# A seventh early set of weight sums, one more pair with seven products, and two sets of sums loaded ahead

## The chip, the cores and the metric

The kernel runs on one core of a Trainium2 chip. The core has a matrix engine (TensorE, PE in the profile), a vector engine (VectorE, DVE), an activation engine (ScalarE, ACT), GpSimd (POOL) and SyncE (SP), which here only issues DMA transfers. The engines run their own instruction streams and wait for one another through semaphores. The metric is the device time of one execution, in microseconds (us), as the median of several runs.

## What is computed

The reference is one layer of a decoder trunk, with 256 tokens, a model width D = 2048 and a branch width E = 4096:

```
h = rmsnorm(x, norm_g)
shift, scale, gate = split(silu(c) @ ada_w + ada_b, 3)
h = h * (1 + scale) + shift
b_gate, c_gate, v, g = split(h @ w_in, 4)        # w_in is 2048 x 16384
u = causal_depthwise_conv(c_gate * v, conv_w)    # three taps
y = b_gate * u * silu(g)                         # 256 x 4096
out = rmsnorm(x + gate * (y @ w_out), final_g)   # w_out is 4096 x 2048
```

All numbers are float32.

## The kernel before

**Products.** Each float32 operand of a large product is split into a high part, rounded to the matrix engine's fp32r format, and a low part, the remainder. ACT makes the high part (a copy, L389 or L1032), DVE the low part (a subtraction, L394 or L1035). A product is then three matmuls: high by high, high by low, low by high.

**Stages.** The kernel makes the conditioning sums and half of the input product's columns first (`plan`, `part`). Then comes the other half (L843): 8 column groups of 8 pieces each, so 64 pieces. A piece loads 1 MB of w_in, ACT and DVE split it, and PE runs 48 matmuls of 128x256 on it. Three tiles each for the raw, high and low parts go round in rings (`w_tile`), so a piece's load goes out when the piece three before it has been split. Beside the first 32 pieces DVE also sums the gate's part of ada_w (`gate_piece`, `gate_sums`, tiles `at_g` and `gacc`). After each piece `early_weights` is called, and counts its calls; L881 calls it once more at the end.

**Output product.** y @ w_out has four parts: the first columns (0 to 1023), the second columns (1024 to 2047) for twelve of the sixteen pairs of row blocks, and two closing parts for the rows of pairs 4 to 7 (`third_products`, `out_mm`). A pair is 2 x 128 rows of w_out by 1024 columns: four blocks of 128x512, b0 to b3. By the ordinary way (`Columns.eight`) a pair takes eight products of 128x128 by 128x512, 24 matmuls. For the pairs in `SEVEN` and `SEVEN_2` it takes seven, 21 matmuls (`Columns.seven`), by Winograd's form of Strassen's scheme. That needs sums of y's blocks (`token_forms`, made once for pairs 8 to 15) and four sums of w_out's blocks: b1 - b0, b2 - b0, b2 + b1 - b0, and b3 minus the third. The sums and the blocks b1 to b3 are split into high and low parts each.

**Where the weight sums come from.** For some pairs DVE makes them on the spot (`sums_of`, three operations). For the units in `UNITS` they are made early, beside the 64 pieces: `EARLY` says at which call of `early_weights` the blocks are loaded, the sums follow one call later, and ACT's queue stores them to DRAM (`store_made`, 1 MB). There are two ways to do it. The ordinary one takes tiles of the raw and low rings (`raw_u`, `sums_u`). The other, for the units in `IN_PLACE`, takes two tiles of 128x1024 that are free at that time (`staged`), sums in place with four operations (`sums_in_place`), and stores three calls after the load; the first two sums then stand in swapped order, which `swapped` undoes.

**Order.** In the output product each engine's order is the written order (`in_order`). Per pair that is: the loads on SyncE (`piece`), the splits on ACT and DVE, the loads of `load_ends(n)`, a step of the first columns' closing (`closing_steps`; none at n = 6), and PE's matmuls. The second columns take their pairs in the order 0, 1, 10, 2, 11, 3, 9, 12, 8, 13, 14, 15, as n = 0 to 11. Their raw blocks and their sums share a ring of four "lo" tiles, high parts a ring of three, low parts a ring of three. A load goes out when DVE has split what stood in its tile. `third_load` and `gated_load` take slots of y's that are finished (`slot`, a pool of 18 places).

Of the kernel before, what the change touches and what calls it, by code (L numbers as in the profile page):

```python
# [30 lines left out]
SLOT = 2048  # L31
# [86 lines left out]
def short_conv_layer(ctx: ExitStack, tc: tile.TileContext, x, c, norm_g, ada_w, ada_b, w_in, conv_w, w_out, final_g, out):  # L118
    nc = tc.nc
# [29 lines left out]
    def w_tile(kind, name, dtype=F32, i=None):  # L149

        if i is None:
            size = 4 if kind in fourth else 3
            i = nth[kind] % size
            nth[kind] = i + 1
        if i == 3:
            return hpool.tile([P, SLOT + 64], dtype, tag=fourth[kind], name=name)[:, 16 : 16 + SLOT]
        return wpool.tile([P, SLOT], dtype, tag=f"{kind}{i}", name=name, bufs=1)
# [253 lines left out]
    def split(raw, n, lo_tag="lo"):  # L411

        return split_lo(raw, n, split_hi(raw, n), lo_tag)
# [82 lines left out]
    sums = {}  # L496
# [238 lines left out]
    EP = 4  # L735
    W = 512
    SEVEN = range(8, 16)
    SEVEN_2 = range(9, 16)
    forms = {}
    ended_silu = [None]  # L740

# [29 lines left out]
        )  # L771

    LAST = (2, 3)
    UNITS = ((0, 15),) + tuple((2 * W, j) for j in (10, 11, 12, 14, 15))
    EARLY = {32 + 4 * i: unit for i, unit in enumerate(UNITS)}
    IN_PLACE = UNITS[0:6:2]
    EARLY.update({55: "gate", 56: ("gated", LAST[0]), 60: ("gated", LAST[1])})
    made = {}
    to_do = []
# [3 lines left out]
    def sums_of(b, s):  # L783

        yield nc.vector.tensor_tensor(  # L785
            out=s[:, 0:2], in0=b[:, 1:3], in1=b[:, 0:1].to_broadcast([P, 2, W]), op=ALU.subtract
        )
        yield nc.vector.tensor_tensor(out=s[:, 2], in0=b[:, 2], in1=s[:, 0], op=ALU.add)
        yield nc.vector.tensor_tensor(out=s[:, 3], in0=b[:, 3], in1=s[:, 2], op=ALU.subtract)  # L789
# [53 lines left out]
    for ct in range(NS, NCT, 2):  # L843
        for q in QUARTERS:
            bank = psum.tile([P, CT, T], F32, tag="mm", name="mm_b")[:, 0:2]
            col = q * E + ct * P
            for kp in range(0, KT, KP):
                raw = raw_tile("raw")
# [55 lines left out]
    def load_ends(n):  # L904

        if n == 1:
            both = hpool.tile([P, TT, HD], F32, tag="b0", name="xr")
            xh.append([both[:, t] for t in range(TT)])
            closing.append(hpool.tile([P, D], F32, tag="b2", name="closing"))
            fourth["lo"] = "b1"  # L910
            load_broadcast(HD, gate_row[0:1, 0:HD])
            load_x(0, 0)
        elif n == 2:
            load_fg(0)
        elif n == 3:
            load_x(0, 1)
        elif n in (5, 6):
            if n == 5:
                xh.append([slot([P, 2 * W], f"xr{t}") for t in range(TT)])
            load_x(1, n - 5)  # L920
        elif n == 7:
            last_gate.append(slot([P, 2 * W], "last_gate"))
            nc.sync.dma_start(last_gate[0], gate_row[0:1, HD:D].partition_broadcast(P))
        elif n == 10:
            thirds.append(third_load(LAST[0]))
        elif n == 11:
            load_fg(1)
            thirds.append(third_load(LAST[1]))

# [5 lines left out]
            load_o(raw, ep * EP + 2 * i, 2, 2 * W, W)  # L935
        return halves_

    def gated_load(ep):
        halves_ = [slot([P, 2 * W], "raw_y") for _ in range(2)]
        for i, raw in enumerate(halves_):  # L940
            nc.sync.dma_start(raw, made["gated", ep][:, i * 2 * W : (i + 1) * 2 * W])
        return halves_

    def split_halves(raws):
# [33 lines left out]
    def weighted(t, c0, n, pr, at):  # L978
# [3 lines left out]
        nc.scalar.activation(pr, r, AF.Square, scale=D**-0.5, accum_out=fsq[:, t, at : at + 1])  # L982
        yield nc.vector.tensor_tensor(out=r, in0=r, in1=closing[0][:, c0 : c0 + n], op=ALU.mult)

    class Columns:


# [5 lines left out]
        def piece(self, n):  # L993


            j, c0 = self.order[n], self.c0
            raw = w_tile("raw" if n == 0 and c0 == 0 else "lo", "raw_o")
            if n == 0 and c0 == 0:
                nth.update({"raw": 0, "lo": 0})
            ready = (c0, j) in made  # L1000
            if ready:
                blocks = raw.rearrange("p (b f) -> p b f", f=W)
                e = 2 * j * P
                nc.sync.dma_start(blocks[:, 1], w_out[0, e : e + P, c0 + W : c0 + 2 * W])
                nc.sync.dma_start(blocks[:, 2:4].rearrange("p b f -> p (b f)"), w_out[0, e + P : e + 2 * P, c0 : c0 + 2 * W])
            else:
                load_o(raw, 2 * j, 2, c0, 2 * W)
            if j in self.in_turn:
                sums = w_tile("lo", "sums_o")
                if ready:  # L1010
                    nc.sync.dma_start(sums, made[c0, j])
                return self.seven(j, raw, sums, ready)
            hi, lo = split(raw, SLOT, "raw")
            return lambda: self.eight(n, j, hi, lo)
# [12 lines left out]
        def seven(self, j, raw, sums, ready):  # L1027


            hi, lo = hi_tile(), lo_tile("raw")  # L1030
            b, s, bh, bl = (v.rearrange("p (b f) -> p b f", f=W) for v in (raw, sums, hi, lo))
            nc.scalar.copy(bh[:, 1:4], b[:, 1:4])  # L1032
            if not ready:
                list(sums_of(b, s))
            nc.vector.tensor_tensor(out=bl[:, 1:4], in0=b[:, 1:4], in1=bh[:, 1:4].bitcast(F32), op=ALU.subtract)  # L1035
            sh, sl = (v.rearrange("p (b f) -> p b f", f=W) for v in split(sums, SLOT, "raw"))
            bank, p1, p6, p75 = self.bank, self.p1, self.p6, self.p75
            opens, last = j == self.in_turn[0], j == self.in_turn[-1]
            swapped = int((self.c0, j) in IN_PLACE)

            def f(i):
                return [forms[j][h][:, i] for h in range(2)]

            def products():
                triple(p1, y_parts(2 * j, 0), bh[:, 1], bl[:, 1], opens, last)
                triple(bank(0, 1), y_parts(2 * j + 1, 0), bh[:, 3], bl[:, 3])
                triple(bank(0, 0), f(3), bh[:, 2], bl[:, 2])
                triple(p75[:, 0], f(2), sh[:, 1 - swapped], sl[:, 1 - swapped], opens, last)
                triple(p75[:, 1], f(0), sh[:, swapped], sl[:, swapped], opens, last)
                triple(p6, f(1), sh[:, 2], sl[:, 2], opens, last)  # L1050
                triple(bank(1, 1), y_parts(2 * j + 1, 1), sh[:, 3], sl[:, 3])

            return products
# [80 lines left out]
    with in_order():  # L1134
        fourth.update({"lo": "b0", "hi": "b1", "raw": "b2"})
        p75 = wide_bank("mm_7")
        wide = [wide_bank("mm_w") for _ in range(TT)]
        first = Columns(
            0, (0, 1, 8, 2, 9, 3, 10, 4, 11, 5, 12, 13, 6, 14, 15, 7), SEVEN,
            lambda t, d: wide[t][:, d], *extra_banks(), p75, True,  # L1140
        )
        for n in range(16):
            if n == 13:
                fourth.clear()
            first.piece(n)()

        second = Columns(2 * W, (0, 1, 10, 2, 11, 3, 9, 12, 8, 13, 14, 15), SEVEN_2, lambda t, d: halves[d][:, t], None, None, None, False)
        products0 = second.piece(0)
        first.gather()
        products1 = second.piece(1)  # L1150
        load_ends(1)
        evict(0)
        halves = [wide_bank("mm_o") for _ in range(2)]
        products0()
        evict(1)
        second.p75 = wide_bank("mm_7")
        second.p1, second.p6 = po = extra_banks()
        products1()
        steps = closing_steps()
        for n in range(2, 12):  # L1160
            products = second.piece(n)
            load_ends(n)
            if n != 6:
                next(steps, None)
            products()
        assert next(steps, None) is None
        gated = [gated_load(LAST[0])]
        third0 = third_piece(LAST[0], thirds[0])
        second.gather()
        third_products(*third0)  # L1170
        third_products(*third_piece(LAST[1], thirds[1]))
        gated.append(gated_load(LAST[1]))
        late = []
        for t, ep in enumerate(LAST):
            hi, lo = split_halves(gated[t])
            move(t)
            low_halves(gated[t], hi, lo)
            late.append((ep, hi, lo))
        for ep, hi, lo in late:
            out_mm(po[0], 0, ep, hi, lo)  # L1180
        third(0)
        third_weighted(0)
        third(1)
        for t in range(TT):
            nc.scalar.activation(ends[t][:, 1], po[t], AF.Square, scale=D**-0.5, accum_out=fsq[:, t, 2:3])
            finish(t)
            if t == 0:
                third_weighted(1)
                for ep, hi, lo in late:
                    out_mm(po[1], 1, ep, hi, lo)  # L1190
# [24 lines left out]
```

## Time and profile before

| | us |
|---|---|
| median of 3 runs (900.93 to 901.40) | 901.32 |
| the profiled execution | 902.04 |
| its span, first to last instruction | 900.3 |
| start of the 64 pieces on PE | 376.0 |
| start of the first columns | 725.7 |
| start of the second columns | 807.3 |
| end of PE's last matmul | 892.7 |

The profile is that of one execution. Its span is 1.7 us shorter than that execution's time, the rest lying before the first and after the last instruction. The four lower rows are from the chain of work that ended last. Engine names and lines are those of the kernel printed above. In a row of the timeline the first number is the start in us from the span's beginning, the second the length; a bracket says how long the engine was idle before and who released it. PE's matmuls overlap one another, so the distance of their starts is their price, not their length.

### The profile page before, as it was taken

Reading aid. Unit: us, or ns where it says so; the run is one execution under the profiler, and the core shown is the slowest. Engines: PE = TensorE matmul, PEld = TensorE weight load, DVE = VectorE, ACT = ScalarE, POOL = GpSimd, SP = SyncE. Lnnn points to the kernel's source line nnn. Section 1 sums busy time; section 2 is a strip of 40 time slices with the busy share of each in tenths; the row PEclk is TensorE's granted clock in tenths of the full one; section 3 lists DMA queues with packets and bytes.
Section 4 is the critical chain, followed back from the end, with each engine's and each line's share of the span. In section 5 each row is a group of like instructions: output and inputs, shape, how many; then the busy total and the mean of one; then the engine's idle time right before and its main releaser. Section 6 shows DMA issues by size and latency. Waiting matters only on the chain.

```text
span 900.3 us, 16556 instructions
## 1 busy us (share of the span) xinstructions
PE 885.1 (98%) x6974; PEld 847.0 (94%) x6974; DVE 698.7 (78%) x704; ACT 492.9 (55%) x441; POOL 94.0 (10%) x108
## 2 busy tenths in 40 slices
PE   7999999999999999999999999999999999999996
PEld 4999999999999999999999999999999988888875
DVE  5899988889888866856965587677767688877986
ACT  6768866665558856644343434344534455455553
POOL 0000000010000223420033002430000000000000
PEclk9999999999999999999999999999999999999999
DMA  9999999999998597876877788999898765489862
GB/s 310 370 370 368 368 331 361 335 365 377 374 322 288 163 293 226 244 223 198 287 235 229 253 288 270 314 303 327 283 314 285 267 234 191 170 300 365 280 258 93
DMA packets 165817, 257.29 MB, mean 286 GB/s; under 512 B 7844, under 2 KB 106756, under 8 KB 164336
## 3 DMA queue, kind: packets, MB, share of 16 engines
q1 hardware_dynamic: 160192, 239.89, 80.3%
q0 software_dynamic: 3840, 7.94, 3.3%
q10 hardware_dynamic: 1712, 8.43, 2.3%
q8 instruction: 54, 0.88, 0.4%
q14 instruction: 19, 0.16, 0.1%
HBM read 237.86 MB, written 10.50 MB: 276 GB/s over the span
## 4 chain that ended last, share of the span: by engine, by line
PE 89%; DMA 5%; DVE 3%; ACT 1%; issue 1%; SPq 0%; ACTq 0%; DVEq 0%
PE mm_s L554 39%; PE mm_b L554 34%; PE mm_w L969 7%; PE mm L969 5%; PE mm_o L969 4%; DMA at<-in_ada_w_dram 2%; DMA raw<-in_sc_w_in_dram 2%; DVE lo L394 1%; ACT hi L389 1%; DMA sums_o<-made 1%; DMA raw_u<-in_sc_w_out_dram 1%; DVE staged L798 0%; PE sum L427 0%; SPq L247 0%; DVE sums_u L785 0%
## 5 line engine op out<-in xcount | busy, mean ns | idle before, releaser
L554 PE MATMUL mm_b<-hT,hi 128*128 128x256 f32 x2048 | 348.5, 276 | 0.0
L554 PE MATMUL mm_s<-hT,hi 128*128 128x256 f32 x2048 | 335.8, 277 | 0.0
L554 PEld LDWEIGHTS mm_b<-hT,hi 128*128 128x128 f32 x2048 | 308.0, 188 | 0.0
L554 PEld LDWEIGHTS mm_s<-hT,hi 128*128 128x128 f32 x2048 | 298.4, 188 | 0.3
L554 PE MATMUL mm_b<-hT,lo 128*128 128x256 f32 x1024 | 283.0, 276 | 0.6 <-DVE lo L394 0.5
L554 PE MATMUL mm_s<-hT,lo 128*128 128x256 f32 x1024 | 261.3, 276 | 0.0
L389 ACT CAST hi<-raw 128x2048 fp32r<-128x2048 f32 (+1 forms) x66 | 123.8, 1875 | 181.2 <-PE mm_b L554 80.4
L394 DVE TENSOR_TENSOR lo<-raw,hi 128x2048 fp32r<-128x2048 f32 (+1 forms) x66 | 149.7, 2269 | 70.1 <-ACT hi L389 68.7
L554 PEld LDWEIGHTS mm_b<-hT,lo 128*128 128x128 f32 x1024 | 192.2, 188 | 1.2 <-DVE lo L394 1.2
L554 PEld LDWEIGHTS mm_s<-hT,lo 128*128 128x128 f32 x1024 | 182.4, 188 | 0.0
L394 DVE TENSOR_TENSOR lo<-raw_s,hi 128x2048 fp32r<-128x2048 f32 (+1 forms) x80 | 148.8, 1866 | 31.0 <-ACT hi L389 30.4
L389 ACT CAST hi<-raw_s 128x2048 fp32r<-128x2048 f32 (+2 forms) x81 | 124.1, 1541 | 68.3 <-PE mm_s L554 44.3
L524 DVE SCALAR_TENSOR_TENSOR gv<-at,silu_c,gv 128x512 f32<-128x512 f32 x105 | 78.8, 750 | 9.0 <-DMA at<-in_ada_w_dram 7.3
L578 ACT COPY acc<-mm_s 128x1024 f32<-128x1024 f32 x54 | 54.5, 1012 | 29.7 <-PE mm_s L554 29.6
L730 POOL TENSOR_TENSOR gacc<-gacc,z 128x512 f32<-128x512 f32 x28 | 48.7, 1741 | 115.9 <-DMA z<-gacc 115.9
L969 PE MATMUL mm_w<-hi,y 128*128 128x512 f32 x160 | 52.0, 389 | 0.0
L724 DVE SCALAR_TENSOR_TENSOR gacc<-at_g,silu_c,gacc 128x512 f32<-128x512 f32 x60 | 45.0, 749 | 6.4 <-DMA at_g<-in_ada_w_dram 5.1
L969 PE MATMUL mm_o<-hi,y 128*128 128x512 f32 x140 | 45.7, 390 | 0.0
L389 ACT CAST hi<-sums_o 128x2048 fp32r<-128x2048 f32 x15 | 28.6, 1910 | 30.8 <-DVE sums_o L789 12.2
L394 DVE TENSOR_TENSOR lo<-sums_o,hi 128x2048 fp32r<-128x2048 f32 x15 | 34.4, 2292 | 13.7 <-ACT hi L389 13.7
L592 ACT COPY mm_s<-acc 128x1024 f32<-128x1024 f32 x38 | 38.6, 1016 | 2.6 <-DVE acc L581 1.8
L394 DVE TENSOR_TENSOR lo<-raw_o,hi 128x2048 fp32r<-128x2048 f32 x13 | 29.8, 2290 | 9.4 <-ACT hi L389 9.4
(191 smaller groups left out, 755.7 us busy)
## 6 DMA issues: line engine op xcount, KB each, us to landing
raw<-in_sc_w_in_dram SPq DMA_DIRECT2D x64, 1024.0 KB, 7.3
raw_s<-in_sc_w_in_dram SPq DMA_DIRECT2D x47, 1024.0 KB, 8.5
at<-in_ada_w_dram SPq DMA_DIRECT2D x126, 256.0 KB, 8.0
raw_o<-in_sc_w_out_dram SPq DMA_DIRECT2D x22, 1024.0 KB, 5.3
raw_s<-in_sc_w_in_dram SPq DMA_DIRECT2D x33, 512.0 KB, 7.2
at_g<-in_ada_w_dram SPq DMA_DIRECT2D x32, 512.0 KB, 8.6
sums_o<-made SPq DMA_DIRECT2D x6, 1024.0 KB, 6.0
raw_u<-in_sc_w_out_dram SPq DMA_DIRECT2D x5, 1024.0 KB, 6.2
```

The source lines that it names most:

```text
L389: last_high[0] = nc.scalar.copy(hi[:, :n], raw[:, :n])
L394: last_low[0] = nc.vector.tensor_tensor(out=lo[:, :n], in0=raw[:, :n], in1=hi[:, :n].bitcast(F32), op=ALU.subtract)
L524: nc.vector.scalar_tensor_tensor(out=gv, in0=at4[:, i], scalar=c_k, in1=gv, op0=ALU.mult, op1=ALU.add)
L554: mm = last_mm[0] = nc.tensor.matmul(dst, w, h[k], start=begins and left, stop=ends, skip_group_check=True)
L578: nc.scalar.copy(acc[ch, q], bank)
L592: nc.scalar.copy(bank, acc[ch, q])
L724: nc.vector.scalar_tensor_tensor(out=ga, in0=at3[:, i, :], scalar=s, in1=ga, op0=ALU.mult, op1=ALU.add)
L730: nc.gpsimd.tensor_tensor(out=ga, in0=ga, in1=turned, op=ALU.add)
L969: nc.tensor.matmul(dst, y[a], b, start=opens and i == 0, stop=ends and i == 2, skip_group_check=True)
```

## The change

```diff
-    SEVEN_2 = range(9, 16)
+    SEVEN_2 = range(8, 16)
...
-    UNITS = ((0, 15),) + tuple((2 * W, j) for j in (10, 11, 12, 14, 15))
-    EARLY = {32 + 4 * i: unit for i, unit in enumerate(UNITS)}
-    IN_PLACE = UNITS[0:6:2]
+    UNITS = ((0, 15),) + tuple((2 * W, j) for j in (8, 10, 11, 12, 14, 15))
+    EARLY = {28 + 4 * i if i else 24: unit for i, unit in enumerate(UNITS)}
+    IN_PLACE = UNITS[0:1] + UNITS[1:6:2]
...
-        elif n == 10:
+        elif n in (9, 10):
+            ahead[2 * W, n + 5] = load_made((2 * W, n + 5))
+        elif n == 11:
             thirds.append(third_load(LAST[0]))
-        elif n == 11:
             load_fg(1)
             thirds.append(third_load(LAST[1]))
...
-    def gated_load(ep):
+    def load_made(unit):
         halves_ = [slot([P, 2 * W], "raw_y") for _ in range(2)]
         for i, raw in enumerate(halves_):
-            nc.sync.dma_start(raw, made["gated", ep][:, i * 2 * W : (i + 1) * 2 * W])
+            nc.sync.dma_start(raw, made[unit][:, i * 2 * W : (i + 1) * 2 * W])
         return halves_
...
             if j in self.in_turn:
+                if (c0, j) in ahead:
+                    return self.seven(j, raw, ahead[c0, j], ready)
                 sums = w_tile("lo", "sums_o")
...
-            sh, sl = (v.rearrange("p (b f) -> p b f", f=W) for v in split(sums, SLOT, "raw"))
+            if isinstance(sums, list):
+                parts = split_halves(sums)
+                low_halves(sums, *parts)
+            else:
+                parts = split(sums, SLOT, "raw")
+            sh, sl = (v.rearrange("p (b f) -> p b f", f=W) for v in parts)
```

- Pair 8 of the second columns goes over from eight products to seven. Its sums are made early, in place.
- The units' calls: (0, 15) moves from 32 to 24, pair 8 takes 32, and the other five stay at 36, 40, 44, 48 and 52. (0, 15), pair 8, pair 11 and pair 14 are made in place.
- The sums of pairs 14 and 15 are loaded by `load_ends(9)` and `load_ends(10)`, one pair ahead, into two slots of y's each, and no longer by `piece` into a tile of the "lo" ring. They are split in halves (`split_halves`, `low_halves`: two operations each on ACT and DVE).
- The first `third_load` moves from n = 10 to n = 11.

More of the change, by code (lines that the diff above doesn't have):

```diff
@@ L983, in weighted @@
         yield nc.vector.tensor_tensor(out=r, in0=r, in1=closing[0][:, c0 : c0 + n], op=ALU.mult)
+    ahead = {}
     class Columns:
@@ L1030, in seven @@
             hi, lo = hi_tile(), lo_tile("raw")
-            b, s, bh, bl = (v.rearrange("p (b f) -> p b f", f=W) for v in (raw, sums, hi, lo))
+            b, bh, bl = (v.rearrange("p (b f) -> p b f", f=W) for v in (raw, hi, lo))
             nc.scalar.copy(bh[:, 1:4], b[:, 1:4])
             if not ready:
-                list(sums_of(b, s))
+                list(sums_of(b, sums.rearrange("p (b f) -> p b f", f=W)))
             nc.vector.tensor_tensor(out=bl[:, 1:4], in0=b[:, 1:4], in1=bh[:, 1:4].bitcast(F32), op=ALU.subtract)
-            sh, sl = (v.rearrange("p (b f) -> p b f", f=W) for v in split(sums, SLOT, "raw"))
+            if isinstance(sums, list):
[4 more added lines that the diff above has]
+            sh, sl = (v.rearrange("p (b f) -> p b f", f=W) for v in parts)
             bank, p1, p6, p75 = self.bank, self.p1, self.p6, self.p75
@@ L1166, in short_conv_layer @@
         assert next(steps, None) is None
-        gated = [gated_load(LAST[0])]
+        gated = [load_made(("gated", LAST[0]))]
         third0 = third_piece(LAST[0], thirds[0])
@@ L1171, in short_conv_layer @@
         third_products(*third_piece(LAST[1], thirds[1]))
-        gated.append(gated_load(LAST[1]))
+        gated.append(load_made(("gated", LAST[1])))
         late = []
```

## The prediction

> **What bounds the kernel now.** I read the busy shares first, then the waits of TensorE (PE), then the chain that ended last, and only then the timelines of the two stretches that the change touches. The page's busy list and its chain by engine:
>
> ```profile
> PE 885.1 (98%) x6974; PEld 847.0 (94%) x6974; DVE 698.7 (78%) x704; ACT 492.9 (55%) x441; POOL 94.0 (10%) x108
> ...
> PE 89%; DMA 5%; DVE 3%; ACT 1%; issue 1%; SPq 0%; ACTq 0%; DVEq 0%
> ```
>
> PE is busy for 98% of the span, so time can go in two ways only: fewer matmuls, or fewer waits of PE. The view of waits lists what PE waited for (total us, times, longest); two lines lie in this change's stretches:
>
> ```profile
> PE mm L969 <- DVE lo L394: 1.9, 2, 1.7
> ...
> PE mm_b L554 <- DVE lo L394: 0.5, 2, 0.3
> ```
>
> The first is the output product, the second the input product. Here is the price of one 128x512 matmul, and the start of the input product's last 64 pieces, from the chain (start, length, count):
>
> ```profile
> 376.01 173.98 PE mm_b L554 x1535
> ...
> 870.21 11.56 PE mm_o L969 x51
> ```
>
> 11.56/51 = 0.227 us a matmul. 173.98/1535 x 48 = 5.44 us a piece, so piece n begins at 376.01 + 5.4375 n. PE's timeline in the second columns (start, length):
>
> ```profile
> 843.65 0.39 PE L969 MATMUL mm<-hi,y 128*128 128x512 f32 x1
> ...
> 853.88 0.39 PE L969 MATMUL mm<-hi,y 128*128 128x512 f32 x1
> ...
> 856.57 0.50 PE L969 MATMUL mm<-lo,form 128*128 128x512 f32 x1 [0.25 <-DVE lo L394]
> ...
> 863.96 0.39 PE L969 MATMUL mm<-hi,y 128*128 128x512 f32 x1
> ...
> 868.10 0.50 PE L969 MATMUL mm<-lo,form_h 128*128 128x512 f32 x1 [1.70 <-DVE lo L394]
> ...
> 870.50 0.62 PE L969 MATMUL mm_o<-hi,y 128*128 128x512 f32 x2
> ```
>
> Pair 12 opens at 843.65 and has 21 matmuls, so pair 8 opens at 848.41 and, with 24, ends at 853.88, where pair 13 opens. Pair 15 opens at 863.96, waits 1.70 us at its eleventh matmul, and ends at 870.73 (the row of 870.50 holds its last matmul and the next piece's first).
>
> **The waits' cause.** Pair 15's sums are the cause of the 1.70 us. SyncE's issues, and then ACT's splits:
>
> ```profile
> 838.32 3.06 SPq L768 DMA_DIRECT2D raw_o<-in_sc_w_out_dram  x2
> ...
> 856.54 0.33 SPq L1011 DMA_DIRECT2D sums_o<-made  x1
> ```
>
> ```profile
> 843.85 1.91 ACT L389 CAST hi<-raw_o 128x2048 fp32r<-128x2048 f32 x1 [1.07 <-PE mm_o L969]
> ...
> 863.81 1.91 ACT L389 CAST hi<-sums_o 128x2048 fp32r<-128x2048 f32 x1 [2.93 <-DMA sums_o<-made]
> ```
>
> The load goes out at 856.54, when VectorE (DVE) has finished with the "lo" tile that it overwrites, and ACT gets it at 863.81. DVE's timeline around it (start, length, line, what idled before it):
>
> ```profile
> 845.02 1.22 DVE L976 TENSOR_TENSOR xr<-xr,z 128x1024 f32<-128x1024 f32 x1
> 846.15 2.29 DVE L394 TENSOR_TENSOR lo<-raw_o,hi 128x2048 fp32r<-128x2048 f32 x1
> 848.36 1.22 DVE L983 TENSOR_TENSOR xr<-xr,closing 128x1024 f32<-128x1024 f32 x1
> 849.49 1.22 DVE L785 TENSOR_TENSOR sums_o<-raw_o 128x1024 f32<-128x1024 f32 x1
> ...
> 852.08 1.75 DVE L1035 TENSOR_TENSOR lo<-raw_o,hi 128x1536 fp32r<-128x1536 f32 x1
> 854.22 2.29 DVE L394 TENSOR_TENSOR lo<-sums_o,hi 128x2048 fp32r<-128x2048 f32 x1 [0.39 <-ACT hi L389]
> 856.43 1.75 DVE L1035 TENSOR_TENSOR lo<-raw_o,hi 128x1536 fp32r<-128x1536 f32 x1
> 858.10 2.29 DVE L394 TENSOR_TENSOR lo<-sums_o,hi 128x2048 fp32r<-128x2048 f32 x1
> 860.91 1.76 DVE L1035 TENSOR_TENSOR lo<-raw_o,hi 128x1536 fp32r<-128x1536 f32 x1 [0.53 <-ACT hi L1032]
> 865.75 2.29 DVE L394 TENSOR_TENSOR lo<-sums_o,hi 128x2048 fp32r<-128x2048 f32 x1 [3.08 <-ACT hi L389]
> 867.96 2.35 DVE L953 TENSOR_TENSOR lo<-raw_y,hi 128x1024 fp32r<-128x1024 f32 x2
> ```
>
> Two things are to be seen. DVE has a hole of 3.08 us ahead of pair 15's sums. But from 845.02 to 856.43 it is full but for 0.39 us, and it feeds pair 13 with nothing to spare: the low halves of pair 13's blocks end at 853.83, and PE wants them one matmul after 853.88.
>
> **Part one: pair 8 with seven products.** It removes three matmuls, 3 x 0.227 = 0.68 us. On DVE the one split of 2.29 us becomes a split of the three blocks (1.75) and one of the sums (2.29). By start-to-start steps of these rows, 1.67 is added (856.43 to 858.10). ACT gets one more split and has room. DVE's order is written out by hand, so everything behind pair 8 slides. I walk it:
>
> - Pair 8's blocks: DVE 846.15 to 847.82. ACT splits them from 843.85; the "hi" tile for the sums comes free with pair 12's ninth matmul (843.65 + 9 x 0.227 = 845.7, about 845.9 with its drain), so ACT ends at about 847.85.
> - Pair 8's sums: DVE 847.9 to 850.1; PE wants them at 848.41 + 10 x 0.227 = 850.7. No wait.
> - Closing step L983 to 851.25; pair 13's sums (849.49 to 852.08, 2.59) to 853.85; its blocks to 855.55.
> - PE ends pair 8 at 848.41 + 21 x 0.227 = 853.17 and wants pair 13's low halves at 853.40: **a new wait of 2.2 us**. ACT splits pair 13's sums 853.9 to 855.8, DVE 855.85 to 858.1; PE wants them at 857.7: 0.4 more. The eleventh matmul starts at 858.15; in before it started at 856.57, so pair 13 closes 1.6 us later than now, at 860.8 (859.2 now).
>
> **Part two: the sums of 14 and 15 ahead.** SyncE issues them behind the blocks of pairs 13 and 14, into slots of finished y's. Each is split in halves: 2.35 us on DVE instead of 2.29 (row 867.96). DVE is then ready with pair 14's blocks at 859.8, its sums at 862.2, pair 15's blocks at 864.2, its sums at 866.6. PE wants these at 861.0, 863.1, 865.8 and 867.9. The 1.70 us are gone, and pairs 14 and 15 run 4.76 each: 860.8 + 9.52 = 870.3, against 870.73 now. **These two parts give 0.4 us**, of the 0.68 + 1.70 + 0.25 = 2.6 that PE alone would allow. The rest goes into the wait at pair 13. Behind 870 DVE is about as early as before, so the 0.4 reaches the end.
>
> **Part three: the seventh set, early.** The two 512 KB loads go out behind piece 24's load, about 484 (the split at 508.44 is piece 26's, as shown below; piece 24's load follows piece 21's split, 5 x 5.44 us ahead of that split's end). The old load's place at piece 32 now serves pair 8 and costs what it cost. New are the loads, four DVE operations, and a 1 MB store on ACT's queue behind piece 27's split. The windows by piece (length, busy of PE, PEld, DVE, ACT, POOL, clock, DMA share, GB/s); the group of DVE's operation on `staged` (ns, least, median, most); DVE's rows; and SyncE's:
>
> ```profile
> 501.10:506.50 5.40, 5.40 (x50) 5.40 (x49) 2.29 (x1) 1.87 (x2) 0.00 (x0) 1.00 0.61 196
> 506.50:511.90 5.40, 5.40 (x50) 5.40 (x49) 5.14 (x8) 2.94 (x3) 0.00 (x0) 1.00 0.92 276
> 511.90:517.40 5.50, 5.50 (x50) 5.50 (x50) 2.79 (x5) 1.91 (x1) 0.00 (x0) 1.00 1.04 360
> 517.40:522.80 5.40, 5.40 (x50) 5.40 (x49) 5.02 (x6) 2.40 (x2) 0.00 (x0) 1.00 0.81 263
> 522.80:528.30 5.50, 5.50 (x51) 5.50 (x51) 2.20 (x2) 1.97 (x2) 0.00 (x0) 1.00 0.96 320
> ```
>
> ```profile
> L798 DVE TENSOR_TENSOR staged<-staged x12: 680/684/692, 554.1 to 643.5; 128x512 f32<-128x512 f32 x12
> ```
>
> ```profile
> 508.44 2.29 DVE L394 TENSOR_TENSOR lo<-raw,hi 128x2048 fp32r<-128x2048 f32 x1
> ...
> 528.86 1.54 DVE L724 SCALAR_TENSOR_TENSOR gacc<-at_g,silu_c,gacc 128x512 f32<-128x512 f32 x2 [3.86 <-DMA at_g<-in_ada_w_dram]
> 530.32 2.28 DVE L394 TENSOR_TENSOR lo<-raw,hi 128x2048 fp32r<-128x2048 f32 x1
> ...
> 558.99 2.28 DVE L394 TENSOR_TENSOR lo<-raw,hi 128x2048 fp32r<-128x2048 f32 x1
> ```
>
> ```profile
> 532.63 0.37 SPq L849 DMA_DIRECT2D raw<-in_sc_w_in_dram  x1
> ```
>
> The loads are wanted by 505 and have DMA engines at 0.61 before that, so they cost nothing. The four operations are 4 x 0.684 = 2.7 us of DVE from about 505. They push the split at 508.44 by 2.7 at worst, to an end at 513.4; it serves piece 26, which begins at 517.4. Hidden, with 4 us left; without that cover they would cost 2.7. The store meets full DMA engines (1.04). 1.05 MB at that window's 360 GB/s are 2.9 us, which loads in flight pay. The next window has 0.19 x 5.4 = 1.0 us free, so 1.9 us are left for the gate's load that DVE already waits 3.86 us for at 528.86. Behind that in DVE's order is the split at 530.32, which ends at 532.60, just ahead of SyncE's load at 532.63 into the tile that it freed. That is piece 32's, so the split is piece 29's. PE wants it at 376.01 + 29 x 5.4375 + 0.23 = 533.9: 1.3 us of margin, and a wait of 1.9 - 1.3 = 0.6. The ends are 0, if the store falls into gaps, and 2.9, if the delay lasts to piece 34: its split (558.99) ends at 561.3 and its products begin at 376.01 + 34 x 5.4375 + 0.2 = 561.1, with no margin at all. Below nothing there is no end, since nothing is taken away ahead of piece 32. I take 0.6: the row nearest the store is the split with the 1.3 us.
>
> The sum: -0.4 + 0.6 = **+0.2 us**. The profiled execution took 902.04 (span 900.3), which would be 902.2. The runs' median is 901.32, 0.7 lower; the same difference gives 901.5, which I predict.
>
> **The rivals.**
>
> - *The whole 2.6 us* (898.7, or 899.3 with the 0.6). This needs DVE to be ready for pair 13 at 853.4. For it speaks the hole of 3.08 us; against it, that the hole lies behind pair 13 and the order is fixed. Chance 0.10.
> - *Slower by the store's backlog.* The delay of 2.9 us is not worked off before piece 34, since the windows to 528 are 0.8 to 1.0 full, and PE pays it all: 901.3 - 0.4 + 2.9 = 903.8. It decides from a delay of 2.2 us there (1.8 beside the 0.4). Against it speaks that some share is free in most windows. [...] Chance 0.14.
> - *Pair 8's sums come late.* They go out when the tile of pair 9's sums is free, about 841, where SyncE's second load of the row at 838.32 goes now. Two rows of the DMA view (KB, us to landing), the issues at 832.93 and at 812.91:
>
> ```profile
> sums_o<-made SPq DMA_DIRECT2D x1, 1024.0 KB, 4.8
> ...
> sums_o<-made SPq DMA_DIRECT2D x1, 1024.0 KB, 9.8
> ```
>
>   With 4.8 they are there at 845.8, in time. With 9.8 they land at 850.8 where ACT wants them at 845.9: 4.9 late, DVE and PE with them, 901.5 + 4.9 = 906.4. Chance 0.04.
> - *The sums ahead are not ahead:* the y slots come free only with pair 8, at 853. Pair 14's blocks, queued behind on SyncE, would then land near 858, and DVE be ready at 861, when PE wants them. This costs about nothing and lies inside the forecast.
>
> The forecast has 0.72. This kernel's measurement can tell about 0.2%, 1.8 us, from no change: faster 0.10, within 0.72, slower 0.14 + 0.04 = 0.18. The forecast's own bounds are 0 to 0.9 us gained at the end (a dozen hand-overs of about 0.04 us in the walk, either way), and 0 to 1.6 us for the store (a delay of 2.9 against 1.3): 900.4 to 902.9. To hold 8 in 10 the range reaches part of the way to the first two rivals: 899.8 to 903.4.
>
> **What would show it.** Step one: 21 matmuls for pair 8, and a wait of some 2.2 us at pair 13's second matmul; no wait there means that DVE was not full. Step two: no wait on pair 15's sums. Step three: pieces 29 to 39 begin later by what the store costs; the output product's start, 725.7 in the table above, tells it. The prediction is wrong if that start moves by over 2 us or pair 13 does not wait.

## The result and the profile after

The changed kernel takes 902.55 us (median of 20 runs, 901.29 to 904.40), the kernel before 901.21 in the same comparison (20 runs, 899.35 to 903.09). The ratio is 1.0018, 95% interval 1.0011 to 1.0025: 1.3 us more, where 0.2 more was forecast. Ten of the 20 runs stand between 901.3 and 902.2 and ten between 902.9 and 904.4, which the kernel before does not do. Of all the runs below, three took 1114, 3191 and 4424 us (in kernels 5 and 6 and the kernel before) and are in no ratio. The profiled execution (901.85, span 900.1) is of the lower group.

First the page's busy line of the changed kernel, and its waits of PE (total us, times, longest):

```profile
PE 883.8 (98%) x6971; PEld 846.7 (94%) x6971; DVE 704.6 (78%) x711; ACT 494.6 (55%) x444; POOL 91.4 (10%) x108
```

```profile
PE mm L970 <- DVE lo L1040: 2.4, 1, 2.4
PE mm L970 <- DVE lo L394: 1.1, 2, 0.8
```

The 1.7 us at pair 15 are gone, and a wait of 2.4 us has come, on the split of a pair's blocks (L1040, L1035 before). PE's three waits, and then DVE's timeline from pair 12's sums on:

```profile
850.31 0.50 PE L970 MATMUL mm<-lo,gate 128*128 128x512 f32 x1 [0.77 <-DVE lo L394]
...
855.70 0.51 PE L970 MATMUL mm<-lo,y 128*128 128x512 f32 x1 [2.37 <-DVE lo L1040]
...
858.37 0.50 PE L970 MATMUL mm<-lo,form 128*128 128x512 f32 x1 [0.30 <-DVE lo L394]
```

```profile
843.72 1.22 DVE L977 TENSOR_TENSOR xr<-xr,z 128x1024 f32<-128x1024 f32 x1
844.86 1.75 DVE L1040 TENSOR_TENSOR lo<-raw_o,hi 128x1536 fp32r<-128x1536 f32 x1
847.96 2.29 DVE L394 TENSOR_TENSOR lo<-sums_o,hi 128x2048 fp32r<-128x2048 f32 x1 [1.35 <-ACT hi L389]
850.17 1.22 DVE L984 TENSOR_TENSOR xr<-xr,closing 128x1024 f32<-128x1024 f32 x1
851.31 1.22 DVE L785 TENSOR_TENSOR sums_o<-raw_o 128x1024 f32<-128x1024 f32 x1
...
853.90 1.75 DVE L1040 TENSOR_TENSOR lo<-raw_o,hi 128x1536 fp32r<-128x1536 f32 x1
856.02 2.29 DVE L394 TENSOR_TENSOR lo<-sums_o,hi 128x2048 fp32r<-128x2048 f32 x1 [0.37 <-ACT hi L389]
858.23 1.75 DVE L1040 TENSOR_TENSOR lo<-raw_o,hi 128x1536 fp32r<-128x1536 f32 x1
```

`gate` in PE's first row is the form of pair 8, `y` with L1040 pair 13's first product, `form` pair 13's sums. DVE goes from pair 8 to pair 13 as walked, but for a hole of 1.35 us ahead of pair 8's sums. ACT's row shows whom it waited for, SyncE's when that load went out:

```profile
846.02 1.91 ACT L389 CAST hi<-sums_o 128x2048 fp32r<-128x2048 f32 x1 [1.98 <-DMA sums_o<-made]
```

```profile
839.70 0.33 SPq L1016 DMA_DIRECT2D sums_o<-made  x1
```

Out at 839.70, there at 845.92: 6.2 us, where the walk took 4.8. The early part went another way. The chain of the changed kernel:

```profile
376.42 348.16 PE mm_b L554 x3072
724.58 10.89 PE mm_w L970 x48
...
870.02 11.56 PE mm_o L970 x51
```

All 64 pieces run without a break in 348.16 us. In the profile before they took 725.68 - 376.01 = 349.67, with waits at 583 and 589. From the output product's start to the row of 51 matmuls it is 145.44 now, and was 870.21 - 725.68 = 144.53. So in this pair of profiles the pieces are 1.5 us shorter and the output product 0.9 longer.

### The profile page after: what moved, and what is told of

It is laid out like the page before. It is cut to its first block, busy times and chain, and to the rows that moved or that the text cites. A ratio compares the mean times of both kernels' runs of the same rounds, so it can differ in the third digit from the quotient of the medians.

```text
span 900.1 us, 16572 instructions
## 1 busy us (share of the span) xinstructions
PE 883.8 (98%) x6971; PEld 846.7 (94%) x6971; DVE 704.6 (78%) x711; ACT 494.6 (55%) x444; POOL 91.4 (10%) x108
## 4 chain that ended last, share of the span: by engine, by line
PE 93%; DMA 3%; DVE 2%; ACT 1%; issue 1%; SPq 0%; ACTq 0%
PE mm_s L554 39%; PE mm_b L554 39%; PE mm_w L970 7%; PE mm L970 5%; PE mm_o L970 4%; DMA at<-in_ada_w_dram 2%; ACT hi L389 1%; DVE lo L394 1%; DMA sums_o<-made 1%; DVE sums_o L785 0%; PE sum L427 0%; SPq L247 0%; DVE sums_o L789 0%; DVE sums_o L788 0%; PE tp_g L539 0%
## 5 line engine op out<-in xcount | busy, mean ns | idle before, releaser
L394 DVE TENSOR_TENSOR lo<-raw,hi 128x2048 fp32r<-128x2048 f32 (+1 forms) x66 | 153.2, 2323 | 61.6 <-ACT hi L389 59.3
L730 POOL TENSOR_TENSOR gacc<-gacc,z 128x512 f32<-128x512 f32 x28 | 46.6, 1666 | 122.9 <-DMA z<-gacc 122.9
L389 ACT CAST hi<-sums_o 128x2048 fp32r<-128x2048 f32 x14 | 26.7, 1908 | 29.0 <-DVE sums_o L789 12.4
L970 PE MATMUL mm_o<-hi,y 128*128 128x512 f32 x128 | 42.2, 390 | 0.0
L394 DVE TENSOR_TENSOR lo<-sums_o,hi 128x2048 fp32r<-128x2048 f32 x14 | 32.1, 2292 | 11.5 <-ACT hi L389 11.5
L1037 ACT CAST hi<-raw_o 128x1536 fp32r<-128x1536 f32 x16 | 23.7, 1481 | 26.4 <-PE mm_w L970 14.1
```

The source lines that it names most:

```text
L389: last_high[0] = nc.scalar.copy(hi[:, :n], raw[:, :n])
L394: last_low[0] = nc.vector.tensor_tensor(out=lo[:, :n], in0=raw[:, :n], in1=hi[:, :n].bitcast(F32), op=ALU.subtract)
L730: nc.gpsimd.tensor_tensor(out=ga, in0=ga, in1=turned, op=ALU.add)
L970: nc.tensor.matmul(dst, y[a], b, start=opens and i == 0, stop=ends and i == 2, skip_group_check=True)
```

## The experiments

The two stretches were taken apart. Each kernel was timed against the kernel before on the same chip; the ratios have their 95% intervals. "Pieces" and "output" are from the chain of each profile: the 64 pieces, and the output product up to its first closing part's first matmul (by that mark 145.21 before and 146.12 in the changed kernel).

| kernel | median, us | ratio to before | pieces | output |
|---|---|---|---|---|
| changed | 902.55 | 1.0018 (1.0011 to 1.0025) | 348.16 | 146.12 |
| 1: only 14 and 15 ahead | 899.08 | 0.9981 (0.9972 to 0.9990) | 348.16 | 143.58 |
| 2: nothing ahead | 903.32 | 1.0029 (1.0018 to 1.0039) | 348.16 | 147.76 |
| 3: early set unused | 901.29 | 0.9996 (0.9985 to 1.0007) | 348.41 | 144.46 |
| 4: closing step moved | 900.45 | 0.9997 (0.9988 to 1.0005) | 348.16 | 145.50 |
| 5: pair 8's sums ahead too | 901.30 | 1.0006 (0.9997 to 1.0015) | 349.58 | 144.75 |
| 6: both 4 and 5 | 899.62 | 0.9988 (0.9979 to 0.9997) | 348.16 | 143.68 |
| 7: high parts first | 902.08 | 1.0008 (0.9998 to 1.0018) | 348.16 | 146.16 |
| 8: 4, 5 and 7 | 898.68 | 0.9970 (0.9961 to 0.9980) | 351.39 | 142.59 |
| 9: 1 and 7 | 897.65 | 0.9961 (0.9949 to 0.9974) | 348.16 | 142.33 |
| 10: pair 13 later | 904.28 | 1.0039 (1.0025 to 1.0053) | 348.26 | 147.87 |

### 1: only the sums of pairs 14 and 15 ahead

```diff
-    SEVEN_2 = range(8, 16)
+    SEVEN_2 = range(9, 16)
...
-    UNITS = ((0, 15),) + tuple((2 * W, j) for j in (8, 10, 11, 12, 14, 15))
-    EARLY = {28 + 4 * i if i else 24: unit for i, unit in enumerate(UNITS)}
-    IN_PLACE = UNITS[0:1] + UNITS[1:6:2]
+    UNITS = ((0, 15),) + tuple((2 * W, j) for j in (10, 11, 12, 14, 15))
+    EARLY = {32 + 4 * i: unit for i, unit in enumerate(UNITS)}
+    IN_PLACE = UNITS[0:6:2]
```

> Only the sums of pairs 14 and 15 are loaded ahead; pair 8 keeps eight products and there are six early sets, as in before. Full-vector-engine theory: VectorE's order up to pair 13 is that of before, so PE waits about 0.25 us at pair 13 and no longer 1.70 us at pair 15: 1.7 to 1.9 us faster than before, some 899.4 us, and the spread of its runs is that of before. Rival (the load of the sums was not what ended last, another wait takes its place): within 0.7 us of before.

Measured: 0.9981, that is 1.7 us less than before, as the first theory said. Its profile has one wait on the splits of the second columns left:

```profile
855.41 0.50 PE L970 MATMUL mm<-lo,form 128*128 128x512 f32 x1 [0.24 <-DVE lo L394]
```

So this half of the change does what it should. By the ratios, seven products for pair 8, with its early set, then cost 1.0018 - 0.9981 = 0.37% or 3.3 us, with three matmuls fewer.

### 2: nothing loaded ahead

```diff
-        elif n in (9, 10):
-            ahead[2 * W, n + 5] = load_made((2 * W, n + 5))
-        elif n == 11:
+        elif n == 10:
             thirds.append(third_load(LAST[0]))
+        elif n == 11:
             load_fg(1)
```

> Pair 8 with seven products and the seventh early set, but the sums of pairs 14 and 15 loaded into the lo ring as in before. Full-vector-engine theory: the waits of about 2.4 us at pair 13 and 0.8 at pair 8 stay, and the load of pair 15's sums goes out only when pair 13's sums are split, 1.8 us later than in before (856.5), so a wait of about 2 us comes back at pair 15: 2 us slower than the changed kernel, 904.5 us. Rival (the wait at pair 13 comes from transfers that crowd the queue because of the loads ahead): the wait at pair 13 shrinks below 1 us and the time stays at that of the changed kernel, 902.5 us, or less.

Measured: 1.0029, 1.0 us over the changed kernel, half of what was expected. The wait at pair 13 is the same 2.37 us, so the loads ahead do not make it. At pair 15 PE waits only 0.82, since it comes there late; the rows show why:

```profile
854.76 0.63 PE L969 MATMUL mm<-lo,y 128*128 128x512 f32 x1 [2.37 <-DVE lo L1039]
855.19 0.63 PE L969 MATMUL mm<-hi,y 128*128 128x512 f32 x1
855.62 0.63 PE L969 MATMUL mm_o<-hi,y 128*128 128x512 f32 x1
856.04 0.63 PE L969 MATMUL mm_o<-lo,y 128*128 128x512 f32 x1
...
869.05 0.50 PE L969 MATMUL mm<-lo,form_h 128*128 128x512 f32 x1 [0.82 <-DVE lo L394]
```

Behind the wait the matmuls start every 0.43 us and not every 0.23. From this wait's end to pair 13's first product with low parts of the sums it is 3.75 us (854.76 to 858.51), against 2.67 in the changed kernel's first profile (855.70 to 858.37). The slow matmuls bring PE 1.1 us later to these products. They cost nothing at the end here: pair 15's sums go out only at 857.40, when DVE has split pair 13's, and PE, had it come earlier, would have waited longer for them at 869.05. By the profiles the output product is 1.64 longer than in the changed kernel's first profile, nearer to the 2 us expected than the medians are.

### Two more profiles of the changed kernel

> The changed kernel as it is, for a second profile of it. Its 20 runs fall into two groups, 901.3 to 902.2 and 902.9 to 904.4, and the first profile is one of the lower group. If the early set's transfers make the upper group, a profile of the upper group shows the output product's start (724.6 in the first profile) some 2 us later, with waits of PE in pieces 29 to 40; if the second columns make it, their waits of 3.4 us grow by 2; if neither, PE's rate itself is lower at the same waits, with a lower granted clock.

> As the look before it: a third profile of the changed kernel, with the same three readings.

The second profile (903.40) is of the upper group, the third (902.15) of the lower. The second profile behind pair 13's wait, and its windows (length, busy of PE, PEld, DVE, ACT, POOL, PE's granted clock, DMA share, GB/s):

```profile
856.39 0.79 PE L970 MATMUL mm<-lo,y 128*128 128x512 f32 x1 [2.38 <-DVE lo L1040]
856.98 0.63 PE L970 MATMUL mm<-hi,y 128*128 128x512 f32 x1
857.41 0.63 PE L970 MATMUL mm_o<-hi,y 128*128 128x512 f32 x1
```

```profile
854.00:856.00 2.00, 0.01 (x1) 0.00 (x0) 2.00 (x2) 1.23 (x1) 0.00 (x0) 1.00 1.01 394
856.00:858.00 2.00, 1.61 (x4) 1.33 (x5) 1.63 (x2) 2.00 (x2) 0.00 (x0) 0.53 1.04 413
858.00:860.00 2.00, 2.00 (x7) 1.53 (x6) 2.00 (x2) 0.08 (x2) 0.00 (x0) 0.62 1.03 389
860.00:862.00 2.00, 2.00 (x10) 1.67 (x9) 1.61 (x2) 1.97 (x2) 0.00 (x0) 1.00 1.04 406
```

PE's granted clock falls to a half for some 3 us behind a wait of 2.38 us. The third profile has the same wait of 2.38 and the full clock, like the first. So the third of the three readings holds, in one stretch. The second profile's pieces also took 349.47 us, 1.3 over the least, with a wait of 0.54 at 578. Against the third profile its output product is 1.0 longer (146.55 and 145.56) and its pieces are 1.0 longer (349.47 and 348.50), so in the one profile of the upper group that there is the excess is about half clock, half pieces.

The records of the single runs tell more, since each has PE's mean granted clock over the run. In the profiled runs of all the kernels it is 0.995 or 0.996 in the four whose profile shows the half clock behind pair 13's wait, and 0.997 to 0.999 in the ten others. Of the changed kernel's 20 runs it is 0.996 in nine of the ten upper ones and in three of the ten lower ones, and 0.997 or 0.998 in the rest; of the 72 runs of the kernel before, in the comparisons of kernels 1 to 10, it is below 0.997 in five. So the half clock goes with the upper group, but not without exceptions, and it is not the whole of the 2 us between the groups.

### 3: the early set made and not used

Against the kernel before:

```diff
-    UNITS = ((0, 15),) + tuple((2 * W, j) for j in (10, 11, 12, 14, 15))
-    EARLY = {32 + 4 * i: unit for i, unit in enumerate(UNITS)}
-    IN_PLACE = UNITS[0:6:2]
+    UNITS = ((0, 15),) + tuple((2 * W, j) for j in (8, 10, 11, 12, 14, 15))
+    EARLY = {28 + 4 * i if i else 24: unit for i, unit in enumerate(UNITS)}
+    IN_PLACE = UNITS[0:1] + UNITS[1:6:2]
...
-            ready = (c0, j) in made
+            ready = (c0, j) in made and j in self.in_turn
```

> Before, with the seventh early set made (loaded behind piece 24, summed, stored) but never used: pair 8 of the second columns keeps eight products, nothing is loaded ahead. Theory (the loss lies in the second columns, the early set is hidden): within 0.6 us of before, 901.2 to 901.8, one cluster of runs as in before. Rival (the early set's transfers and sums cost PE time in pieces 24 to 40, and cause the two clusters of runs, near 901.8 and 903.8, that the changed kernel shows): 1.3 us or more slower than before, in two clusters.

Measured: 0.9996 (0.9985 to 1.0007), so the set costs nothing that the median shows. But its 12 runs are spread over 898.2 to 903.3, more than those before. Its profile (899.55) has the pieces at 348.41. The early set was forecast at 0.6. In the eleven profiles with it (the changed kernel's three, and kernels 2 to 8 and 10) the pieces take 348.16 to 351.39, on average 0.6 over the least; in the three without it 0, 0 and 1.5. That does not tell it from nothing. The place tells a little more: in five of the eleven PE loses time at 577 to 579, in piece 37 (0.2 to 1.3 us by the distances of the matmuls' starts), and in none of the three, where the 1.5 are lost at 561, 583 and 589. In the three of the five that lose most there (the second profile and kernels 5 and 8), the chain of work that ended last runs back from there through the added sums at 505. So the early set probably costs such a delay in some runs.

### 4: the last closing step behind pair 13

```diff
-            if n != 6:
+            if n not in (6, 8):
                 next(steps, None)
```

> The changed kernel with one edit: the last closing step of the first columns (one ACT square and one VectorE product of 128x1024, 1.13 us on VectorE) goes from behind pair 8 to behind pair 13. Full-vector-engine theory: PE's wait at pair 13 falls by 1.13 us, from 2.4 to 1.2, and nothing else grows, so 1.1 us faster than the changed kernel, 901.4 us. Rival (pair 13 waits for its loads or for ACT, not for VectorE's turn): the wait and the time stay as in the changed kernel, within 0.3 us.

Measured: 0.9997, 1.9 us less than the changed kernel by the ratios. PE's waits:

```profile
850.55 0.50 PE L970 MATMUL mm<-lo,gate 128*128 128x512 f32 x1 [1.18 <-DVE lo L394]
...
854.81 0.50 PE L970 MATMUL mm<-lo,y 128*128 128x512 f32 x1 [1.22 <-DVE lo L1040]
```

The wait at pair 13 is 1.22, as expected to the tenth, so it was DVE's turn that PE waited for. The wait at pair 8 varies with the load (0.8 in the changed kernel, 1.2 here). By the medians more than 1.1 us came off. That fits the clock: ten of its eleven runs lie within 900.1 to 901.3, all with a mean granted clock of 0.997 or more; the eleventh, 902.47, has 0.996.

### 5 and 6: pair 8's sums ahead too, and with the closing step moved

```diff
             nc.sync.dma_start(last_gate[0], gate_row[0:1, HD:D].partition_broadcast(P))
+            ahead[2 * W, 8] = load_made((2 * W, 8))
```

> The changed kernel with the sums of pair 8 also loaded ahead, behind pair 12's loads, into slots of finished y's and split in halves. Theory (pair 8's sums come 1.4 us too late for VectorE, since their load waits for a lo tile until 839.7): PE's wait of 0.77 us at pair 8 goes, VectorE gains 1.35 us there and PE's wait at pair 13 stays at 2.2 us: 1.4 us faster than the changed kernel, 901.1 us. Rival (ACT or the place of the high part holds the split of pair 8's sums, not the load): the wait at pair 8 stays above 0.5 us and the time within 0.4 us of the changed kernel.

> The same, and the last closing step of the first columns behind pair 13 instead of behind pair 8. Full-vector-engine theory: the wait at pair 13 falls by another 1.1 us to 1.1, so 2.5 us faster than the changed kernel, 900.0 us, and still slower than the version with only pairs 14 and 15 loaded ahead (899.1). Rival (seven products for pair 8 pay once VectorE is relieved a little): 898.6 us or less.

Measured: 1.0006 and 0.9988, so 1.1 and 2.7 us less than the changed kernel, where 1.4 and 2.5 were expected. The wait at pair 8 is gone in both, and that at pair 13 is 2.0 and 0.9 (the longest, third number):

```profile
PE mm L971 <- DVE lo L1041: 2.0, 1, 2.0
```

```profile
PE mm L971 <- DVE lo L1041: 0.9, 1, 0.9
```

Both price the two causes of the late DVE: the load, and the full order. In kernel 5's profile the output product is 1.37 shorter than in the changed kernel's first, as expected, but its pieces are 1.42 longer.

### 7: PE takes what needs only high parts first

```diff
+    def highs_first(*items):
+        for dst, y, hi, lo, opens, ends in items:
+            for i in range(2):
+                nc.tensor.matmul(dst, y[i], hi, start=opens and i == 0, stop=False, skip_group_check=True)
+        for dst, y, hi, lo, opens, ends in items:
+            nc.tensor.matmul(dst, y[0], lo, start=False, stop=ends, skip_group_check=True)
```

The three products of the blocks go through it together, and the four of the sums; the same products are added in another order.

> The changed kernel with PE's products of a pair in another order: for the blocks first the six matmuls that need only high parts and then the three with low parts, for the sums first eight and then four. Full-vector-engine theory: VectorE's times stay, so pair 13's low parts still come at about 855.7 us; the waits of 0.8 at pair 8 and 0.3 at pair 13's sums go, PE reaches pair 13 earlier and waits there about 2.4 us as now, but has 15 matmuls left instead of 20: 1.5 us faster than the changed kernel, 901.0 us, and a second group of runs stays, since the wait does. Rival (PE's order does not matter, since the waits only move): within 0.4 us of the changed kernel.

Measured: 1.0008, 0.9 us less than the changed kernel, not 1.5. The waits at pair 8 and at pair 13's sums went, and the one at pair 13 rose to 2.68, for PE comes earlier. Behind it the clock is at a half in the profile, which takes back what the order gave:

```profile
856.00:858.00 2.00, 2.00 (x5) 1.61 (x6) 1.81 (x1) 2.00 (x3) 0.00 (x0) 0.50 1.03 391
```

### 8 and 9: the best of each kind

Kernel 8 is 4, 5 and 7 together; kernel 9 is 1 and 7, with eight products for pair 8.

> All together: pair 8's sums loaded ahead too, the last closing step behind pair 13, and high parts first. Theory: no wait of PE over 0.3 us is left in the second columns, so the three matmuls saved show: 1.2 us faster than the same without high parts first, 898.4 us, faster than the version with only pairs 14 and 15 ahead (899.1), and no second group of runs. Rival (VectorE stays the bound over the whole stretch): 899.3 us or more.

> Only the sums of pairs 14 and 15 ahead, pair 8 with eight products, six early sets, and high parts first. Theory: the one wait left, 0.24 us at pair 13, goes: 0.3 us faster than without high parts first, 898.8 us. It shows what pair 8's seven products are worth once VectorE keeps up: 0.4 to 0.7 us between this and the version with all together.

Measured: 0.9970 and 0.9961. Kernel 8 is 1.6 us under kernel 6 by the ratios, where 1.2 was expected. Kernel 9 is the fastest of all, 3.5 us less than before, and 1.8 less than kernel 1 by the ratios, where 0.3 was expected: more small waits went than the one I had named. By the starts of the matmuls, kernel 1's profile has three stalls in the second columns (at 808.8, 839.9 and 855.4), 1.2 us together, and kernel 9's has none. Pair 8's seven products are worth nothing even here. Between the two 0.4 to 0.7 us had been expected. Kernel 8's output is 142.59 us with three matmuls fewer, kernel 9's 142.33: by the starts, kernel 8 has three stalls between 855.8 and 861.6, 0.8 us together, which take back the 0.68. Kernel 9 has no wait of PE in the output product that the view of waits lists. In kernel 8 one is left, and its profile (900.90, its slowest run) shows what the pieces can lose:

```profile
PE mm_b L554 <- DVE lo L394: 2.3, 3, 1.0
...
PE mm L978 <- DVE lo L1048: 0.3, 1, 0.3
```

### 10: a longer wait on purpose

```diff
+            if n == 9:
+                for _ in range(2):
+                    nc.vector.tensor_tensor(out=u2, in0=closing[0][:, 0:W], in1=closing[0][:, W : 2 * W], op=ALU.mult)
             products = second.piece(n)
```

> The changed kernel with two more VectorE operations of 128x512 ahead of pair 13's sums (their result is used by nothing), about 1.35 us: PE's wait at pair 13 grows from 2.4 to 3.7 us. Clock theory (a wait of about 2.4 us here lowers PE's granted clock to half in some executions, for some 3.4 us, and that makes the upper group of the changed kernel's runs): with the longer wait it is lowered in nearly all, so one group, 905 us or more, 2.4 or more above the changed kernel's median, and the profile shows a clock of about 0.5 behind the wait. Rival (the groups come from somewhere else): both groups are 1.35 us higher, 903.2 and 905.2, half of the runs in each, and the clock stays 1.0 in half of the profiles.

Measured: 1.0039, five runs between 904.15 and 905.68. The median is 0.7 below what the clock theory named, but no run lies near 903.2. The wait is 3.70 us, and the clock behind it:

```profile
857.09 0.50 PE L970 MATMUL mm<-lo,y 128*128 128x512 f32 x1 [3.70 <-DVE lo L1040]
```

```profile
856.00:858.00 2.00, 0.91 (x4) 0.78 (x5) 1.63 (x2) 2.00 (x2) 0.00 (x0) 1.00 1.03 400
858.00:860.00 2.00, 2.00 (x8) 1.37 (x7) 2.00 (x2) 1.05 (x2) 0.00 (x0) 0.63 1.06 398
860.00:862.00 2.00, 2.00 (x6) 1.58 (x6) 2.00 (x2) 1.71 (x2) 0.00 (x0) 0.51 1.02 402
```

PE starts again at the full clock, which falls 1.45 us later, at 858.54. One profile shows it for one run; the mean granted clock of all five runs, 0.994 to 0.996, says that all had it.

## Why the prediction was right or wrong

- **Part one, the full DVE order: right.** The wait at pair 13 was put at 2.2 and is 2.37, the one at its sums at 0.4 and is 0.30. Kernel 4 shows that it is DVE's turn: 1.13 us taken out of its order took 1.15 from the wait.
- **Part one, "no wait" at pair 8: mis-sized.** The term is the landing of pair 8's sums, taken as 4.8 us and measured as 6.2, 5.8 and 5.6 in the three profiles of the changed kernel. The rival of late sums had the mechanism but put its price at 4.9. PE waits 0.77 there in the first profile, 0.36 in the second and less than the view lists in the third, and DVE has a hole of 0.8 to 1.35 ahead of these sums. Kernel 5 gives its worth: 1.1 us by the ratios.
- **Part two, the sums of 14 and 15 ahead: right.** The 1.70 us went, and no wait came in their place. Alone this is worth 1.7 us (kernel 1).
- **The end, "0.4 us given": wrong in sign.** The output product became 0.9 longer in the first profile, 1.3 and 0.4 in the second and third. Against the forecast the first is 1.3 too long, and taking pair 8's late sums away in kernel 5 takes 1.37 off; the half clock makes the second longer. The walk priced the wait at pair 13 by its length alone and had no term for what follows it: the prediction opened with two ways for time to go, matmuls and waits, and a lower clock is a third.
- **Part three, 0.6 for the store: not confirmed.** The store went out at 512.4 and met DMA engines with a share of 0.43 and 0.80 in the next two windows of 2 us (1.02 and 1.05 in the profile before), since the compiled order had moved the gate's loads behind the added sums, from 505 to 512; the walk had kept the old order. That loads issued before the store would pay for it was an estimate, and these profiles do not show it. The pieces came out at 348.16 to 349.47 in the three profiles of the changed kernel, and kernel 3 is equal to before within 0.15%. The delay at piece 37 that five of the eleven profiles with the set show is too rare here to give it a price; that stays open.
- **The sum: near by chance.** 901.5 was forecast, 902.55 measured, inside the range and inside 0.2% of before. The two terms had the wrong size in opposite directions, and the clock was missing.

The rival of the whole 2.6 us fell as its counter-argument said. The store's backlog did not show in the medians. The slots of y's came free in time.

## What to carry to other kernels

A product saved on the matrix engine is worth nothing where the engine that feeds it is full: here 0.68 us of matmuls asked for 1.67 us of VectorE in a stretch that had none. Before adding work, look at the feeding engine's timeline for holes, and at whether they lie ahead of the place that needs them. Load ahead what arrives last, let the matrix engine take first what needs only the operands that come first, and keep any wait of it short: in these profiles its clock stayed full behind a wait of 1.70 us, and fell to a half at two of the four of 2.37 or 2.38 us.

## What the hardware showed

PE's granted clock fell to a half, for 3.4 us, at one wait in this kernel. It did so in two of four profiles with a wait of 2.37 or 2.38 us (kernel 2 and the changed kernel's second profile), and in those with 2.68 and 3.70. It did not in the profiles whose longest wait there was 2.04 (kernel 5), 1.70 (before), 1.22 and less. Each time the matmuls started every 0.43 us instead of 0.23. PE came 1.1 us later to pair 13's sums in kernel 2, where the wait at pair 15 took this up, and 0.9 in the second profile (856.39 to 860.00, 3.61 instead of 2.67), where it reached the end; this is less than the slow matmuls' own loss because the next wait was hidden.

Here is the fall in kernel 10 (length, busy of PE, PEld, DVE, ACT, POOL, PE's granted clock, DMA share, GB/s):

```profile
855.12:858.54 3.42, 1.45 (x6) 1.24 (x7) 3.05 (x3) 3.06 (x2) 0.00 (x0) 1.00 1.03 398
858.54:861.95 3.41, 3.41 (x9) 2.48 (x9) 3.41 (x3) 2.21 (x3) 0.00 (x0) 0.50 1.04 402
```

The longest wait of PE in the second columns of each of these profiles, and the clock at it. The half clock's times are read from the clock of windows of 1 and 2 us:

| profile | wait, us | its end | half clock |
|---|---|---|---|
| 10 | 3.70 | 857.09 | 858.5 to 862.0 |
| 7 | 2.68 | 855.87 | 855.8 to 859.2 |
| changed, second | 2.38 | 856.39 | 856.1 to 859.5 |
| changed, third | 2.38 | 855.98 | none |
| 2 | 2.37 | 854.76 | 855.0 to 858.4 |
| changed, first | 2.37 | 855.70 | none |
| 5 | 2.04 | 855.41 | none |
| before | 1.70 | 868.10 | none |

So it is not the wait's length alone that decides: of the four waits of 2.37 or 2.38 us two had the half clock and two did not. Nor did the fall keep one distance from the wait: it came 0.3 us ahead of its end in the second profile, 0.2 behind it in kernel 2, and 1.45 behind it in kernel 10. What else decides is left open here. In the records of the single runs, 12 of the changed kernel's 20 runs have a mean granted clock of 0.996, and so have five of kernel 5's ten, though its one profile has the full clock.
